# The expert loop's weights in fewer, larger transfers, in another order

## The chip, the cores and the metric

The kernel runs on one core of a Trainium2 chip. The metric is device time in microseconds. Engine names are those of the profile: PE is TensorE's matmul, PEld its weight load, DVE VectorE, ACT ScalarE, POOL GpSimd, SP SyncE; SPq is SyncE's sequencer, which issues transfers.

## The reference

One layer of a backbone over 2048 latent tokens of 1024 columns and 256 context tokens: an input projection, neighbourhood attention in 8 heads, a bidirectional mLSTM in 4 heads, an output projection, and a mixture of 64 experts, of which each token uses two. All in float32. The change touches how the experts' weights come in (and, for their room, how attention names its tiles). What the experts compute:

```python
def expert_block(args):
    tok, e = args
    xb = xt[jnp.minimum(tok, n_tok - 1)]
    return (jax.nn.silu(xb @ w1[e]) * (xb @ w3[e])) @ w2[e]     # w1, w3: 1024x512, w2: 512x1024
```

An expert's three matrices are 2.1 MB each, 6.29 MB together, and 64 experts are 403 MB.

## The kernel before, in words

The kernel runs its stages one after another: input projection, mLSTM, attention, output projection with routing, the expert loop, a last normalisation. Attention keeps each head's operands in one of two pools: per head the tiles q, ka and kb (query, key high and low part) and bias0, bias1, bias2, each with three bias blocks. The output projection puts its weights into the even pool's tiles once they are free, and the expert loop then uses the same memory for expert weights.

The loop takes the experts' tokens in units. Each of its 28 iterations has two half-steps (u = 0 and u = 1), 56 in all, counted here from 0. A half-step computes one unit of the **wide lane** (64 tokens of an expert with many, `l = 0`) and one of the **narrow lane** (32 tokens, `l = 1`). On TensorE its order is: `hidden(1, u)`, the narrow unit's products with w1 and w3 in eight steps k of 128 rows; `hidden(0, u)`, the wide unit's (L2011 both); the transposes of the next tokens (L1975); `output(1, u)` and `output(0, u)`, the products with w2 in four pieces c (L2043). The result is scattered by GpSimd with an accumulating indirect transfer (L2054).

The wide lane has one set of weights, `W[0]`: w1 and w3 in the tiles mask (k 0 to 3), q (k 4, 5) and ka (k 6, 7), w2 in mo, mo, mo, xo. The narrow lane has two, used in turn: `W[1]` for u = 0 (kb, bias0, bias1, bias2; xo, xo, w2_1_2, w2_1_3) and `W[2]` for u = 1 (tiles w13_2_* and w2_2_*, shown as w). In half-step h SyncE issues the loads of the wide lane's next weights, which half-step h+1 uses, and of the narrow lane's, which half-step h+2 uses. A load waits until TensorE has read the old contents of its tile. Each has a condition: where the next unit belongs to the same expert, the transfer is left out, but the instruction still stands in SyncE's queue, makes its waits, and then counts its completion semaphore up itself, for TensorE waits on that all the same.

SyncE works in order. Its order in a half-step was: the narrow lane's first half of w1 and w3 (four transfers of 0.52 MB, `load13`, L1097), the wide lane's first half (four), the narrow lane's second half (four), the wide lane's second half (four), then w2 of the narrow lane (four, `load2`, L1102) and of the wide lane (four): 24. The scheduler gives SyncE's transfers eight completion semaphores in rotation, and a transfer waits until the one that had its semaphore before has landed. With 24 in a half-step, the four narrow ones of a group always share their semaphores with the narrow groups before and behind them. Which expert comes next SyncE reads from a table in SBUF (`coming`, TENSOR_LOAD, two values for each lane).

```python
                e1, f1 = coming(1, u)
                e0, f0 = coming(0, u)
                for c in (0, 2):
                    load13(e1, (c, c + 1), f1)
                    load13(e0, (c, c + 1), f0)
                ...
                load2(e1, f1)
                load2(e0, f0)
```

Of the kernel before, what the change touches and what calls it, by code (L numbers as in the profile page):

```python
# [35 lines left out]
def tile_layer(ctx, tc, A, out):  # L36
# [666 lines left out]
    def head(h):  # L703

        pair, f0 = h // 2, (h % 2) * 64
        kp = kps[h % 2]
        q = kp.tile([P, SEQ], F32R, name="q")
        ka = kp.tile([P, NT], F32R, name="ka")
        kb = kp.tile([P, NT], F32R, name="kb")
        load(q[0:64, :].bitcast(F32), qhi_d[pair][f0 : f0 + 64, :])  # L710
        yield
        load(q[64:P, :].bitcast(F32), qlo_d[pair][f0 : f0 + 64, :])
        yield
        for dst, src in ((ka, khi_d), (kb, klo_d)):
            for p0 in (0, 64):
                load(dst[p0 : p0 + 64, :].bitcast(F32), src[pair][f0 : f0 + 64, :])
            yield
        bias = []

        def masked(i):  # L720
            w = (12, 16, 12)[i // 3] * 32
            in_order(nc.gpsimd.tensor_tensor(bias[i][:, 0:w], bias[i][:, 0:w], mask[:, i, 0:w], OP.add))  # L722

        for i in range(9):
            rt, ct = i // 3, i % 3
            if ct == 0:
# [4 lines left out]
            t = t3[:, ct, :]  # L731
# [177 lines left out]
    with ExitStack() as es:  # L909
# [12 lines left out]
        def out_weights(k):  # L922

            raw = raws[k]
            if k % 2 == 0:
                n_ = ("mask", "q", "ka", "kb")[k // 2]
                if n_ == "mask":
                    pair_ = kps[0].tile([P, 4, D], F32R, name=n_)
                    spare.append(pair_)
                else:  # L930
                    pair_ = kps[0].tile([P, 2, D], F32R, name=n_)
                pairs.append(pair_)
            hi, lo = pairs[k // 2][:, 0], pairs[k // 2][:, 1]
            if k % 2:
                if k == 1:
                    hi, lo = pairs[0][:, 2], pairs[0][:, 3]
                else:
                    t3 = kps[0].tile([P, 2, D], F32R, name=f"bias{k // 2 - 1}")
                    hi, lo = t3[:, 0], t3[:, 1]
            in_order(nc.scalar.copy(hi, raw[:]))  # L940
# [4 lines left out]

        pairs, spare, raws = [], [], []

# [151 lines left out]
    def load2(e, fl=None, chunks=range(4)):  # L1099
        for i in chunks:  # L1100
            s_ = A["w2"][0, e[0], i * P : (i + 1) * P, :].rearrange("o p n -> p (o n)")
            in_order(nc.sync.dma_start(e[1][1][i][:], s_, cond=fl))  # L1102

# [4 lines left out]
    with ExitStack() as es:  # L1108
# [517 lines left out]
        def first_rows(l, chunks):  # L1626
# [3 lines left out]
            for c in chunks:  # L1630
                W[l][1].append(xi.tile([P, D], F32, name="mo" if l == 0 and c < 3 else "xo"))
            load2(ahead_[l], chunks=chunks)

# [46 lines left out]

        both_ = kps[0].tile([P, 2, 2, 2, 512], F32, name="mask")
        for l, tags in enumerate((("q", "ka"), ("kb", "bias0", "bias1", "bias2"))):
            w13 = [both_[:, 0], both_[:, 1]] if l == 0 else []
            w13 += [kps[0].tile([P, 2, 2, 512], F32, name=n)[:] for n in tags]
            W[l][0].extend(w13)
        for e in ahead_:
            load13(e, range(4))
        first_rows(1, (1,))
# [53 lines left out]
    with ExitStack() as es:  # L1742
        sp = es.enter_context(tc.tile_pool(name="ro_s", bufs=1, reuse_waits="tile"))
        pp = es.enter_context(tc.tile_pool(name="ro_p", bufs=1, space=PSUM, reuse_waits="tile"))
        load2(ahead_[1], chunks=(2, 3))
        e = (ds(nc.values_load(fi[0:1, 2:3], engines=SPE, min_val=0, max_val=63), 1), W[2])
        load13(e, range(4))
        for l, G, c0 in ((0, 2, 0), (1, 4, 512)):
# [205 lines left out]
    wp = moe.enter_context(tc.tile_pool(name="mo_w2", bufs=1, reuse_waits="tile"))  # L1954
    W[2][1].extend(wp.tile([P, D], F32, name=f"w2_2_{i}") for i in range(4))
    load2(e)


    with ExitStack() as es:
# [37 lines left out]
        with tc.For_i(0, n_it, 1, iteration_sync="reg_based") as it:  # L1997
# [3 lines left out]
            def hidden(l, u, between=None):  # L2001
                n, t0 = ((64, 0), (32, 64))[l]
                G = P // n
                w13 = W[0 if l == 0 else 1 + u][0]
                NH = 512 // G
                ph = pp.tile([P, 2, NH], F32, name=f"ph{l}")
                for k in range(KC):
                    if k == 4 and between:
                        between()
                    for j in range(G):  # L2010
                        in_order(nc.tensor.matmul(  # L2011
                            ph[j * n : (j + 1) * n], xT[u][:, k, t0 : t0 + n], w13[k // 2][:, :, k % 2, j * NH : (j + 1) * NH],
                            start=k == 0, stop=k == KC - 1, tile_position=(0, j * n),
                        ))
# [15 lines left out]
            def output(l, u, m, part=None):  # L2030
# [3 lines left out]
                NY = D // G  # L2034
                w2t = W[0 if l == 0 else 1 + u][1]
                gT = gts[l, u]
# [39 lines left out]
            for u in range(2):  # L2076
# [146 lines left out]
```

## Time and profile before

| | us |
|---|---|
| median of 3 runs | 2878.04 (2877.48 to 2882.16) |
| the profiled execution: time | 2883.94 |
| the profiled execution: span | 2882.1 |
| TensorE busy in it | 2525.8 |
| the expert loop in it, first to last product | 1158.8 (1649.1 to 2807.9) |

The span is the time from the first to the last instruction of the profiled execution, the time is what the device counted for the same execution. Times in rows are microseconds from the span's start. A row of a timeline joins several instructions of the same kind; its second number runs from the first one's start to the last one's end.

### The profile page before, as it was taken

The numbers are of one execution on the slowest core, as the hardware profiler recorded it, in microseconds if no ns is written. First come the engines' busy times: TensorE is split into PE (matmuls) and PEld (weight loads), VectorE is DVE, ScalarE is ACT, GpSimd is POOL, SyncE is SP. The second block draws the span as 40 slices with busy tenths as digits, with TensorE's granted clock in tenths as the row PEclk, the third lists the DMA queues.
The fourth block names the chain that finished last, engine by engine and source line by source line (L and its number), as shares of the span: only waits on it lengthen the run. The fifth ranks groups of instructions, "written<-read, shape, count | busy, mean of one in ns | idle before, by whom it ended". The sixth has DMA issues, their size and how long they took to land. (4 is left out here: it accounts for less than half of the span.)

```text
span 2882.1 us, 53652 instructions
## 1 busy us (share of the span) xinstructions
PE 2525.8 (88%) x17276; PEld 1592.8 (55%) x17276; DVE 1235.1 (43%) x2493; ACT 782.0 (27%) x1693; POOL 862.5 (30%) x927
## 2 busy tenths in 40 slices
PE   8999999999977999988988498978998999979890
PEld 4878578777877777776766333323333333323330
DVE  5456135274159865656799721111211211211125
ACT  4333115242145655554543200000000000000004
POOL 1202210011145345455766421212221222212126
PEclk9999999999989999999999599989999999989895
DMA  8634853335299777877544899999597888988926
GB/s 269 163 114 133 276 166 109 121 118 161 93 215 267 203 172 187 187 186 196 149 126 123 271 326 317 312 351 303 168 330 254 272 277 250 339 284 266 338 77 248
DMA packets 361806, 628.05 MB, mean 218 GB/s; under 512 B 82680, under 2 KB 146156, under 8 KB 358604
## 3 DMA queue, kind: packets, MB, share of 16 engines
q1 hardware_dynamic: 329868, 565.92, 61.5%
q0 software_dynamic: 31216, 60.03, 9.2%
q8 instruction: 70, 1.15, 0.2%
q10 hardware_dynamic: 592, 0.46, 0.1%
q14 instruction: 60, 0.49, 0.1%
HBM read 948.05 MB, written 97.42 MB: 363 GB/s over the span
## 5 line engine op out<-in xcount | busy, mean ns | idle before, releaser
L2054 POOL DMA_INDIRECT acc_d<-y,ids x112 | 174.3, 1557 | 670.9 <-DVE y L2051 363.5
L2011 PE MATMUL ph<-mask,xT 128*64 128x512 f32 x896 | 219.3, 632 | 53.6 <-DMA mask<-in_w_dram 53.5
L2017 DVE TENSOR_TENSOR sg<-sg,ph 128x128 f32<-128x128 f32 x112 | 39.6, 354 | 512.3 <-ACT sg L2016 512.3
L2016 ACT ACTIVATE sg<-ph 128x128 f32<-128x128 f32 x112 | 37.0, 330 | 801.2 <-PE ph L2011 590.3
L246 PE MATMUL ps<-xhi,whi 128*128 128x512 f32 (+1 forms) x576 | 221.7, 386 | 1.6 <-DVE ev L509 1.6
L248 PE MATMUL ps<-xhi,wlo 128*128 128x512 f32 (+1 forms) x576 | 220.2, 382 | 0.2 <-DVE wlo L235 0.2
L247 PE MATMUL ps<-xlo,whi 128*128 128x512 f32 (+1 forms) x576 | 220.4, 383 | 0.0
L2011 PE MATMUL ph<-q,xT 128*64 128x512 f32 x448 | 125.3, 685 | 55.7 <-DMA q<-in_w_dram 55.5
L255 PE MATMUL ps<-whi,xhi 128*128 128x512 f32 x416 | 166.1, 400 | 1.4 <-ACT whi L234 1.4
L256 PE MATMUL ps<-wlo,xhi 128*128 128x512 f32 x416 | 164.3, 396 | 3.1 <-DVE wlo L235 3.1
L2011 PEld LDWEIGHTS ph<-mask,xT 128*64 128x64 f32 x896 | 65.3, 143 | 182.4 <-issue 177.3
L972 DVE CUSTOM_DVE_ANT_0 sb<-ps,bias 128x640 f32<-128x640 f32 (+1 forms) x128 | 113.9, 890 | 121.3 <-PE ps L969 106.7
L257 PE MATMUL ps<-whi,xlo 128*128 128x512 f32 x416 | 164.8, 397 | 0.0
L2043 PE MATMUL py<-mo,gT 128*64 128x512 f32 x672 | 158.3, 601 | 6.1 <-DMA mo<-in_w_dram 4.7
L2051 DVE SCALAR_TENSOR_TENSOR y<-py,wgt,g2r 128x256 f32<-128x256 f32 x112 | 69.1, 617 | 220.4 <-PE py L2043 220.4
L1967 POOL DMA_INDIRECT xb<-h_d,idg x58 | 58.1, 1002 | 273.9 <-PE py L2043 251.2
L2027 DVE COPY gT<-pg 128x128 f32<-128x128 f32 x112 | 40.1, 358 | 212.7 <-PE pg L2025 211.5
L246 PEld LDWEIGHTS ps<-xhi,whi 128*128 128x128 f32 x576 | 108.3, 188 | 28.4 <-issue 3.2
L248 PEld LDWEIGHTS ps<-xhi,wlo 128*128 128x128 f32 x576 | 108.3, 188 | 23.3 <-DVE wlo L235 0.6
L247 PEld LDWEIGHTS ps<-xlo,whi 128*128 128x128 f32 x576 | 108.4, 188 | 22.7 <-DVE xlo L182 0.5
L980 ACT ACTIVATE sb<-sb,nm 128x640 f32<-128x640 f32 (+1 forms) x128 | 113.2, 884 | 19.1 <-DVE nm L972 15.3
L722 POOL TENSOR_TENSOR bias<-bias,mask 128x384 f32<-128x384 f32 (+1 forms) x72 | 78.1, 1100 | 119.3 <-DMA bias<-rel_d 119.3
(576 smaller groups left out, 5361.7 us busy)
## 6 DMA issues: line engine op xcount, KB each, us to landing
w<-in_w_dram SPq DMA_DIRECT2D x406, 512.0 KB, 8.1
mask<-in_w_dram SPq DMA_DIRECT2D x228, 512.0 KB, 6.3
bias<-in_w_dram SPq DMA_DIRECT2D x174, 512.0 KB, 11.3
mo<-in_w_dram SPq DMA_DIRECT2D x171, 512.0 KB
xo<-in_w_dram SPq DMA_DIRECT2D x115, 512.0 KB
q<-in_w_dram SPq DMA_DIRECT2D x114, 512.0 KB
ka<-in_w_dram SPq DMA_DIRECT2D x114, 512.0 KB
kb<-in_w_dram SPq DMA_DIRECT2D x58, 512.0 KB
```

What stands on the lines that cost most here:

```text
L246: nc.tensor.matmul(ps, wh_, xhi[g, k][:], start=k == 0, stop=False)
L247: nc.tensor.matmul(ps, wh_, xlo[g, k][:], start=False, stop=False)
L248: nc.tensor.matmul(ps, wl_, xhi[g, k][:], start=False, stop=k == KC - 1)
L255: nc.tensor.matmul(ps, xh, his[k], start=k == 0, stop=False)
L256: nc.tensor.matmul(ps, xh, los[k], start=False, stop=False)
L257: nc.tensor.matmul(ps, xl, his[k], start=False, stop=k == KC - 1)
L722: in_order(nc.gpsimd.tensor_tensor(bias[i][:, 0:w], bias[i][:, 0:w], mask[:, i, 0:w], OP.add))
L972: in_order(nc.vector.tensor_tensor_reduce(out=sb[:, 0:L], in0=ps[:, off:768], in1=bt[:, 0:L], scale=-0.125, scalar=3.0e38, op0=OP.add, op1 ...
L980: in_order(nc.scalar.activation(sb[:, 0:L], sb[:, 0:L], AF.Exp, bias=nm[:], scale=-1.0, accum_out=rss[n // 8][:, n % 8 : n % 8 + 1]))
L2011: in_order(nc.tensor.matmul(ph[j * n : (j + 1) * n], xT[u][:, k, t0 : t0 + n], w13[k // 2][:, :, k % 2, j * NH : (j + 1) * NH], start=k == ...
L2043: in_order(nc.tensor.matmul(py[j * n : (j + 1) * n, :], gT[:, b_, j_ * n : (j_ + 1) * n], w2t[c][:, j * NY : (j + 1) * NY], start=c == 0, ...
L2054: sc = nc.gpsimd.indirect_dma_start(out=acc_d[:].rearrange("t (g n) -> (t g) n", g=G), out_offset=bass.IndirectOffsetOnAxis(ap=ids[u][:, l ...
```

## The change

Attention's q, ka and kb become one tile qkk of the same size, and bias0 to bias2 one tile bias. With these the expert lanes' weights lie in larger pieces. The wide lane's w1 and w3 are two pieces of four k (mask, and the first part of qkk) in place of one of four k loaded in two parts and two of two k. `W[1]` has one piece of four k (bias) and two of two k (bias, and the rest of qkk), with the last two c of w2 in one piece. `W[2]` has two pieces of four k and two w2 pieces of two c. A transfer carries one matrix of one piece: 1.05 MB for four k or for two c. The wide lane's w2 stays in four. A half-step issues 17 transfers at u = 0 (nine narrow, eight wide) and 14 at u = 1 (six and eight), 31 an iteration in place of 48. The wide lane's w1 and w3 now stand as a whole behind the narrow lane's first piece, and the narrow lane's other pieces behind them. The loads ahead of the loop are cut in the same way.

```diff
@@ attention, head(h) @@
-        q = kp.tile([P, SEQ], F32R, name="q")
-        ka = kp.tile([P, NT], F32R, name="ka")
-        kb = kp.tile([P, NT], F32R, name="kb")
+        qkk = kp.tile([P, SEQ + 2 * NT], F32R, name="qkk")
+        q, ka, kb = qkk[:, 0:SEQ], qkk[:, SEQ : SEQ + NT], qkk[:, SEQ + NT :]
...
-            if ct == 0:
-                t3 = kp.tile([P, 3, 768], F32, name=f"bias{rt}")
+            if i == 0:
+                b9 = kp.tile([P, 9, 768], F32, name="bias")
...
@@ load13, load2 @@
-        for i in chunks:
+
+        k = 0
+        for i, t in enumerate(e[1][0]):
+            n = t.shape[2]
             for q, src in enumerate(("w1", "w3")):
-                s_ = A[src][0, e[0], i * 256 : (i + 1) * 256, :].rearrange("o (k p) n -> p (o k) n", p=P)
-                in_order(nc.sync.dma_start(e[1][0][i][:, q], s_, cond=fl))
...
+                if i in chunks:
+                    s_ = A[src][0, e[0], k * P : (k + n) * P, :].rearrange("o (k p) n -> p (o k) n", p=P)
+                    in_order(nc.sync.dma_start(t[:, q], s_, cond=fl))
+            k += n
...
@@ the lanes' tiles @@
-        both_ = kps[0].tile([P, 2, 2, 2, 512], F32, name="mask")
-        for l, tags in enumerate((("q", "ka"), ("kb", "bias0", "bias1", "bias2"))):
-            w13 = [both_[:, 0], both_[:, 1]] if l == 0 else []
-            w13 += [kps[0].tile([P, 2, 2, 512], F32, name=n)[:] for n in tags]
-            W[l][0].extend(w13)
+        m_, q_, b_ = (kps[0].tile([P, n * 1024], F32, name=t) for t, n in (("mask", 4), ("qkk", 6), ("bias", 6)))
+        for l, t, k, n in ((0, m_, 0, 4), (0, q_, 0, 4), (1, b_, 0, 4), (1, b_, 4, 2), (1, q_, 4, 2)):
+            W[l][0].append(t[:, k * 1024 : (k + n) * 1024].rearrange("p (q k n) -> p q k n", q=2, n=512))
...
-    W.append(([wp.tile([P, 2, 2, 512], F32, name=f"w13_2_{i}") for i in range(4)], []))
-    W[1][1].extend(wp.tile([P, D], F32, name=f"w2_1_{i}") for i in range(2, 4))
+    W.append(([wp.tile([P, 2, 4, 512], F32, name=f"w13_2_{i}")[:] for i in range(2)], []))
+    W[1][1].append(wp.tile([P, 2, D], F32, name="w2_1")[:])
...
-    W[2][1].extend(wp.tile([P, D], F32, name=f"w2_2_{i}") for i in range(4))
+    W[2][1].extend(wp.tile([P, 2, D], F32, name=f"w2_2_{i}")[:] for i in range(2))
...
@@ the loop @@
                 e1, f1 = coming(1, u)
+                load13(e1, (0,), f1)
                 e0, f0 = coming(0, u)
-                for c in (0, 2):
-                    load13(e1, (c, c + 1), f1)
-                    load13(e0, (c, c + 1), f0)
+                load13(e0, (0, 1), f0)
+                load13(e1, (1, 2), f1)
```

SyncE's queue shows both halves of the edit. First the w1 and w3 loads of a half-step with u = 0, from the end of the narrow lane's first piece on (kb and bias are narrow, mask and q wide; ISA and REGISTER_ALU set registers). Before:

```order
L1097 DMA bias_14485<-in_w_dram 128x2x512
L1097 ISA
L1097 DMA mask<-in_w_dram 128x2x512
L1097 ISA
L1097 DMA mask<-in_w_dram 128x2x512
L1097 ISA
L1097 DMA mask<-in_w_dram 128x2x512
L1097 ISA
L1097 DMA mask<-in_w_dram 128x2x512
L1097 ISA
L1097 DMA bias_14486<-in_w_dram 128x2x512
```

The same place in the changed kernel (its load13 is at L1089; bias is narrow, mask and qkk wide, until the second bias):

```order
L1089 DMA bias<-in_w_dram 128x4x512
L1089 ISA
L1089 DMA mask<-in_w_dram 128x4x512
L1089 ISA
L1089 DMA mask<-in_w_dram 128x4x512
L1089 ISA
L1089 REGISTER_ALU
L1089 DMA qkk<-in_w_dram 128x4x512
L1089 ISA
L1089 DMA qkk<-in_w_dram 128x4x512
L1089 ISA
L1089 DMA bias<-in_w_dram 128x2x512
```

Four transfers between the narrow lane's pieces were half of the wide lane's w1 and w3, and four are now all of it.

Second, where u = 0 ends and u = 1 begins in SyncE's queue (xo is the last piece of the wide lane's w2, w_2_0 the first of the narrow lane's at u = 1). Before:

```order
L1102 DMA xo<-in_w_dram 128x1024
L2073 ISA
L2073 TENSOR_LOAD items
L2073 ISA x2
L2072 ISA
L2072 TENSOR_LOAD items
L2072 ISA x2
L2073 ISA
L2073 TENSOR_LOAD items
L2073 ISA x2
L1097 ISA
L1097 DMA w_2_0_14713<-in_w_dram 128x2x512
```

In the changed kernel:

```order
L1099 REGISTER_ALU
L1099 DMA xo<-in_w_dram 128x1024
L1089 ISA
L1089 DMA w_2_0_14667<-in_w_dram 128x4x512
L1089 ISA
L1089 DMA w_2_0_14667<-in_w_dram 128x4x512
```

The three table reads that stood between the half-steps have gone to the iteration's head, where all eight now stand before the first transfer (five did).

## Rows read from the trace of the kernel before

**Rows 1.** The page: busy time by engine, then two lines of the span in 40 slices of 72 us: the busy tenths of TensorE and the mean busy tenths of the 16 DMA engines.

```profile
PE 2525.8 (88%) x17276; PEld 1592.8 (55%) x17276; DVE 1235.1 (43%) x2493; ACT 782.0 (27%) x1693; POOL 862.5 (30%) x927
...
PE   8999999999977999988988498978998999979890
...
DMA  8634853335299777877544899999597888988926
```

**Rows 2.** Busy time of each engine by window (us; PE, PEld, DVE, ACT, POOL), then the granted TensorE clock as a share of full speed, the DMA engines' mean busy share and GB/s. The first two are the loop's first and last stretch, the other three lie inside the loop.

```profile
1649.00:1997.00 348.00, 303.89 (x2480) 119.86 (x2480) 60.02 (x160) 20.83 (x40) 64.27 (x47) 0.93 0.95 322
...
2650.00:2808.00 158.00, 135.03 (x1085) 52.20 (x1077) 26.50 (x70) 8.47 (x17) 27.80 (x20) 0.91 0.67 221
1850.00:1900.00 50.00, 34.58 (x276) 13.50 (x276) 5.98 (x16) 2.60 (x5) 6.68 (x5) 0.86 1.01 350
2550.00:2600.00 50.00, 33.51 (x277) 12.94 (x277) 7.00 (x18) 1.07 (x4) 6.13 (x5) 0.80 1.02 360
1660.00:1760.00 100.00, 99.01 (x859) 39.37 (x859) 21.74 (x57) 6.25 (x13) 22.14 (x16) 1.00 0.98 325
```

**Rows 3.** TensorE in order of time at chosen places (start us, us, engine, line, operation out<-in, shapes, count): the first product of half-steps 0, 16, 17, 18, 25, 31, 38, 44 and 49 (nine of 56), and the last products of the loop.

```profile
1649.08 1.93 PE L2011 MATMUL ph<-kb,xT 128*32 128x256 f32 x16 [1.05 <-DVE xT L1978]
...
1997.42 0.85 PE L2011 MATMUL ph<-kb,xT 128*32 128x256 f32 x12
...
2015.20 1.07 PE L2011 MATMUL ph<-w,xT 128*32 128x256 f32 x16
...
2032.98 1.07 PE L2011 MATMUL ph<-kb,xT 128*32 128x256 f32 x16
...
2164.32 1.06 PE L2011 MATMUL ph<-w,xT 128*32 128x256 f32 x14
...
2285.05 1.29 PE L2011 MATMUL ph<-w,xT 128*32 128x256 f32 x20
...
2418.06 1.07 PE L2011 MATMUL ph<-kb,xT 128*32 128x256 f32 x16
...
2538.59 1.07 PE L2011 MATMUL ph<-kb,xT 128*32 128x256 f32 x16
...
2649.84 1.50 PE L2011 MATMUL ph<-w,xT 128*32 128x256 f32 x24
...
2806.82 1.03 PE L2043 MATMUL py<-xo,gT 128*64 128x512 f32 x4
```

**Rows 4.** Who waited for whom in the loop, 1649 to 2808 us: TensorE's three longest waits for transfers (us in total, times, longest us).

```profile
PE ph L2011 <- DMA q<-in_w_dram: 55.5, 17, 7.9
PE ph L2011 <- DMA mask<-in_w_dram: 53.5, 19, 11.2
...
PEld ph L2011 <- DMA q<-in_w_dram: 31.9, 12, 4.6
```

**Rows 5.** SyncE's DMA queue in order of time in half-steps 3 to 5 (start us, us from the first issue to the end of the last, count). On L1097 w is of the narrow lane, mask and q of the wide one; on L1102 xo x1 is the wide lane's last piece; kb is the narrow lane's first piece of half-step 4.

```profile
1717.99 2.61 SPq L1097 DMA_DIRECT2D w<-in_w_dram  x4
1720.99 1.42 SPq L1097 DMA_DIRECT2D mask<-in_w_dram  x4
1722.89 4.17 SPq L1097 DMA_DIRECT2D w<-in_w_dram  x4
...
1734.56 0.07 SPq L1102 DMA_DIRECT2D xo<-in_w_dram  x1
1739.03 1.08 SPq L1097 DMA_DIRECT2D kb<-in_w_dram  x2
...
1757.30 0.07 SPq L1102 DMA_DIRECT2D xo<-in_w_dram  x1
1759.84 2.61 SPq L1097 DMA_DIRECT2D w<-in_w_dram  x4
...
1764.74 6.02 SPq L1097 DMA_DIRECT2D w<-in_w_dram  x4
1771.21 0.50 SPq L1097 DMA_DIRECT2D q<-in_w_dram  x2
```

**Rows 6.** TensorE in half-step 6 (the bracket is idle time before, and what ended it).

```profile
1763.43 3.65 PE L2011 MATMUL ph<-mask,xT 128*64 128x512 f32 x16 [0.26 <-DMA mask<-in_w_dram]
...
1771.83 3.68 PE L2011 MATMUL ph<-q,xT 128*64 128x512 f32 x8 [4.49 <-DMA q<-in_w_dram]
```

**Rows 7.** SyncE's own waits in the loop: the longest in total (us in total, times, longest us).

```profile
SPq L1097 <- DMA w<-in_w_dram: 45.1, 59, 2.3
```

**Rows 8.** The wide lane around half-step 38: its first product on TensorE, SyncE's issue of the next weights into the same tile, and the first wide product of half-step 39.

```profile
2421.66 2.79 PE L2011 MATMUL ph<-mask,xT 128*64 128x512 f32 x12
...
2438.92 2.50 SPq L1097 DMA_DIRECT2D mask<-in_w_dram  x4
...
2444.70 3.68 PE L2011 MATMUL ph<-mask,xT 128*64 128x512 f32 x8 [5.18 <-DMA mask<-in_w_dram]
```

**Rows 9.** SyncE's issue of the wide lane's first pieces in the first and the last of the seven half-steps in which they are loaded (10, 14, 22, 25, 38, 44, 49).

```profile
1872.69 2.61 SPq L1097 DMA_DIRECT2D mask<-in_w_dram  x4
...
2676.11 2.73 SPq L1097 DMA_DIRECT2D mask<-in_w_dram  x4
```

**Rows 10.** DMA queues in the loop, 1649 to 2808 us: packets, MB, share of 16 engines (q1 is SyncE's, q0 that of the indirect transfers).

```profile
q1 hardware_dynamic: 126940, 290.69, 70.1%
q0 software_dynamic: 22295, 33.18, 14.6%
```

More of the change, by code (lines that the diff above doesn't have):

```diff
@@ L730, in head @@
             off = rel.offset + ((ct * 16) * 8 + h) * 23 * 32 + i0 * 32
-            t = t3[:, ct, :]
+            t = b9[:, i, :]
             in_order(nc.gpsimd.memset(t[:, nr * 32 :], 0.0))
@@ L924, in out_weights @@
             raw = raws[k]
[L925 to L939, printed above, removed]
+            if k in (0, 2, 5):
+                t = kps[0].tile([P, 3 if k else 2, 2, D], F32R, name={0: "mask", 2: "qkk", 5: "bias"}[k])
+                pairs.extend((t[:, i, 0], t[:, i, 1]) for i in range(t.shape[1]))
+            hi, lo = pairs[k]
             in_order(nc.scalar.copy(hi, raw[:]))
@@ L944, in low_part @@
             in_order((nc.gpsimd, nc.vector)[k % 2].tensor_tensor(wlo[KO[k]], raws[k][:], whi[KO[k]].bitcast(F32), OP.subtract))
-        pairs, spare, raws = [], [], []
+        pairs, raws = [], []
         def raw_weights(k):
@@ L1093, in load13, with load2 @@
     def load13(e, chunks, fl=None):
-        for i in chunks:
+        k = 0
+        for i, t in enumerate(e[1][0]):
+            n = t.shape[2]
             for q, src in enumerate(("w1", "w3")):
-                s_ = A[src][0, e[0], i * 256 : (i + 1) * 256, :].rearrange("o (k p) n -> p (o k) n", p=P)
-                in_order(nc.sync.dma_start(e[1][0][i][:, q], s_, cond=fl))
[L1099 to L1102, printed above, removed]
+                if i in chunks:
+                    s_ = A[src][0, e[0], k * P : (k + n) * P, :].rearrange("o (k p) n -> p (o k) n", p=P)
+                    in_order(nc.sync.dma_start(t[:, q], s_, cond=fl))
+            k += n
+    def load2(e, fl=None, pieces=range(4)):
+        c = 0
+        for i, t in enumerate(e[1][1]):
+            n = t.shape[1]
+            if i in pieces:
+                s_ = A["w2"][0, e[0], c * P : (c + n) * P, :].rearrange("o (c p) n -> p (o c) n", p=P)
+                in_order(nc.sync.dma_start(t, s_, cond=fl))
+            c += n
     ro_es = ExitStack()
@@ L1630, in first_rows @@
             for c in chunks:
-                W[l][1].append(xi.tile([P, D], F32, name="mo" if l == 0 and c < 3 else "xo"))
-            load2(ahead_[l], chunks=chunks)
+                W[l][1].append(xi.tile([P, 1, D], F32, name="mo" if l == 0 and c < 3 else "xo")[:])
+            load2(ahead_[l], pieces=chunks)
         ahead_ = []
@@ L1679, in tile_layer @@
                 first_experts()
-        both_ = kps[0].tile([P, 2, 2, 2, 512], F32, name="mask")
-        for l, tags in enumerate((("q", "ka"), ("kb", "bias0", "bias1", "bias2"))):
-            w13 = [both_[:, 0], both_[:, 1]] if l == 0 else []
-            w13 += [kps[0].tile([P, 2, 2, 512], F32, name=n)[:] for n in tags]
-            W[l][0].extend(w13)
+        m_, q_, b_ = (kps[0].tile([P, n * 1024], F32, name=t) for t, n in (("mask", 4), ("qkk", 6), ("bias", 6)))
+        for l, t, k, n in ((0, m_, 0, 4), (0, q_, 0, 4), (1, b_, 0, 4), (1, b_, 4, 2), (1, q_, 4, 2)):
+            W[l][0].append(t[:, k * 1024 : (k + n) * 1024].rearrange("p (q k n) -> p q k n", q=2, n=512))
         for e in ahead_:
-            load13(e, range(4))
+            load13(e, range(3))
         first_rows(1, (1,))
@@ L1744, in tile_layer @@
         pp = es.enter_context(tc.tile_pool(name="ro_p", bufs=1, space=PSUM, reuse_waits="tile"))
-        load2(ahead_[1], chunks=(2, 3))
+        load2(ahead_[1], pieces=(2,))
         e = (ds(nc.values_load(fi[0:1, 2:3], engines=SPE, min_val=0, max_val=63), 1), W[2])
-        load13(e, range(4))
+        load13(e, range(2))
         for l, G, c0 in ((0, 2, 0), (1, 4, 512)):
@@ L2003, in hidden @@
                 G = P // n
-                w13 = W[0 if l == 0 else 1 + u][0]
+                w13 = [t[:, :, k] for t in W[0 if l == 0 else 1 + u][0] for k in range(t.shape[2])]
                 NH = 512 // G
@@ L2011, in hidden @@
                         in_order(nc.tensor.matmul(
-                            ph[j * n : (j + 1) * n], xT[u][:, k, t0 : t0 + n], w13[k // 2][:, :, k % 2, j * NH : (j + 1) * NH],
+                            ph[j * n : (j + 1) * n], xT[u][:, k, t0 : t0 + n], w13[k][:, :, j * NH : (j + 1) * NH],
                             start=k == 0, stop=k == KC - 1, tile_position=(0, j * n),
@@ L2034, in output @@
                 NY = D // G
-                w2t = W[0 if l == 0 else 1 + u][1]
+                w2t = [t[:, i] for t in W[0 if l == 0 else 1 + u][1] for i in range(t.shape[1])]
                 gT = gts[l, u]
```

## The prediction

> **What bounds the kernel now.** I read the page first, then windows, then single waits. The page says that TensorE is busy for 88% of the span and that in the loop, from slice 22 on, the DMA engines are at eight or nine tenths in most slices [rows 1]. Neither is full, so the question is what each waits for. The starts of the half-steps answer it [rows 3]: half-step 17 takes 2032.98 - 2015.20 = 17.78 us, which is TensorE's own pace, and 56 of them would be 995.7 us. The loop takes from 1649.1 to 2807.9, 1158.8 us. So **163 us** are lost in it. From the same rows, each stretch less 17.78 us for each half-step: A (0 to 15) 63.8, B (16 to 24) 6.9, C (25 to 30) 14.1, D (31 to 37) 8.6, E (38 to 43) 13.9, F (44 to 48) 22.4, G (49 to 55) 33.5.
>
> The waits name the cause [rows 4]: nearly all are for q and mask, the wide lane's w1 and w3. Yet the wide lane is loaded in only seven half-steps (SyncE's issues tell it: four loaded ones of mask take 2.6 or 2.7 us [rows 9], four left out 1.42 [rows 5]). Over the whole loop SyncE's queue moves 290.7 MB [rows 10], 46 loads of 6.29 MB: 39 narrow, 7 wide. Half-step 6 shows how a load that moves nothing stalls TensorE. SyncE gets to q of half-step 5 at 1771.21, only because four narrow transfers stand before it and take from 1764.74 on, and TensorE resumes at 1771.83 after 4.49 us idle [rows 5, 6]. The reader should see there that SyncE is **late**: it comes to q when TensorE already stands at it in the next half-step.
>
> Why it is late: in half-steps 3 and 4, with narrow loads alone, it needs 21.0 us a turn (1717.99, 1739.03, 1759.84 [rows 5]), where TensorE needs 17.78. Its own work is the larger part. Four loaded issues take 1720.99 - 1717.99 = 3.0 us, 0.75 each; four left out take 1.42 from the first one's start to the last one's end, (1.42 - 0.07) / 3 = 0.45 each, 0.07 being the one left out alone at 1734.56; the gaps with the table reads are 1739.03 - 1734.56 = 4.5 and 1759.84 - 1757.30 = 2.5 us. An iteration has 24 x 0.75 + 24 x 0.45 + 7.0 = 35.8 us of this, 17.9 a half-step, and the rest, 3 us, is waiting for transfers: its three longest kinds of wait are for narrow loads, led by 45.1 us in 59 times [rows 7]. As narrow groups share four semaphores, each narrow transfer waits for the fourth narrow one before it, so 2.1 MB are under way at most.
>
> **The change, part by part.**
>
> *Fewer issues.* With narrow loads alone an iteration becomes 15 x 0.75 + 16 x 0.45 + 7.0 = 25.5 us, 12.7 a half-step, 5.1 less, and below 17.78. SyncE then runs with TensorE until transfers hold it. A 1.05 MB issue is not in the trace; I take 0.75 for it (below: nothing excludes 0.7, above: twice, 1.5, which gives an iteration of up to 36.7 us and SyncE as late as now).
>
> *Order.* The wide lane's first issue stands behind two narrow ones, and a left-out q no longer stands behind a whole narrow w1 and w3. The rotation over eight stays, but with 17 and 14 the groups no longer meet on the same four semaphores, so 4 MB and more can be under way. One wait remains: a wide first piece gets the semaphores of the last narrow w2 transfers of the half-step before, so it waits for that load's end.
>
> *What this is worth.* I go by bytes, since SyncE no longer decides. A load is 6.29 MB and the indirect transfers are 33.2 / 56 = 0.59 MB a half-step [rows 10]. The rate is not known for the new sizes. Below: 325 GB/s, the window of narrow loads alone [rows 2], 19.4 us a load and 1.8 for the scatter. Above: 350, the lower of two windows with wide and narrow loads together, where eight transfers are under way (the other has 360), 18.0 and 1.7. Each stretch at 350, and at 325:
> A: SyncE's issues give 14 narrow and 2 wide loads whose arrival half-step 15 needs, less 6.0 us for the last w2: 16 x 18.0 + 15 x 1.7 - 6.0 = 307.5 us. It starts 8 us after 1649.1 (7.0 of reads, all at the head now, and 1.0 to the first byte). Behind the last byte 1.0 us of signalling and 10.4 of products remain: 17.78 less 3.65 for mask [rows 6] and less the narrow lane's 3.6, from 2418.06 [rows 3] to 2421.66 [rows 8]. The end is at 1976 and not 1997.4: 21.5 us gained. At 325: nothing.
> B, D, E: one wide load each in B and E, none in D. Half-step 38 shows what is lost: its first mask product starts at 2421.66, SyncE's issue comes 17.3 us later, and half-step 39 begins its wide lane at 2444.70 after 5.18 us idle [rows 8]. Issued when the piece is free, 3.7 us after its first product, and with up to 2 us of the narrow load before it, the two pieces are there after 3.7 + 2 + 12.0 + 1.0 = 18.7 us; the first is wanted after 17.78, and needs only half of these bytes. All of it goes: 6.9 + 8.6 + 13.9 = 29.4, by either rate.
> C: both lanes at half-step 25. 4 us to the first byte, two loads and the scatter 39.4, 1.9 for the signal and the last w2 product: 45.3 for two half-steps, 9.7 over 35.56, so 4.4 gained (1.5).
> F: a narrow load goes before, 5.9 us into half-step 44; 47.2 us for two half-steps, 11.6 over, 10.8 gained (6.4).
> G: with half-steps 47 and 48 before it, four loads: 4 + 72 + 6.8 + 1.9 = 84.7 for four half-steps, 13.6 over 71.1, 19.9 gained (14.1).
> Sum: **86** at 350 and **51** at 325. I take the middle, 69, because stretch A is of the narrow kind while C, F and G are of the other.
>
> *Larger pieces.* A piece of 2.1 MB must land whole before its first product, and after it four k remain and not two: 1.9 us (half of mask's 3.65, [rows 6]) in each of four stalls that stay, -7 (below: 0; above: also 3.0 us for the extra 1.05 MB at 350, in seven wide loads, -34). Earlier freeing is lost too, 1.8 us a piece, but while SyncE came 17 us late that was no cover anyone used.
>
> *At nothing.* The joined attention tiles: the loads of a head start only after the last scores of the head two before, as each old tile's last reader was in that last block too. If that were wrong, each of six heads would start its loads later by what one bias tile had been free earlier. The loads before the loop: the loop's first product waits for DVE and not for a transfer, as the bracket at 1649.08 has it [rows 3].
>
> 2883.9 - 69 + 7 = 2822 for the profiled execution; this stood 5.9 over the median, so **2816** for the median.
>
> [...]
>
> **The rivals.**
> *Bytes alone bound it.* In stretch A the DMA engines are 95% busy, in the narrow window 98% [rows 2], so SyncE may be late because it waits for them. For it: the waits of [rows 7]. Against it: stretch G with 67%, and the stall of 39. Then B, D and E keep their losses, A gives nothing, and only the order at double loads (C, F, G at 325: 22) remains: about 2856.
> *Slower.* The large pieces decide: SyncE stays late, since issue time grows with size, and every wide load must come whole. Price: 7 x (3.0 + 1.9 + 1.8) = 47, so 2925 with no gain beside it. It decides if SyncE still issues mask over about 12 us after its first product. Against it: four loaded issues of w13 took 3.0 us at 0.52 MB, which is time per instruction as much as per byte.
> *More.* The DMA engines run well above 360 GB/s with more under way and slack carries over between stretches: waits of 40 remain of 163, 2878 - 123 = 2755.
> *It does not do what it says.* A semaphore rotation that still ties wide to narrow makes it the same as before, 2878.
>
> **How the numbers follow.** The forecast has 0.70, with a range of its own from 2783 to 2845 (86 and a little over, 51 less the 7 and a little under). Bytes alone 0.11, more 0.06, no change 0.05, slower 0.08. A measurement can tell about 0.2%, 6 us, from no change. Faster is 0.70 + 0.11 + 0.06 = 0.87, same 0.05, slower 0.08. The range goes from 2783 to 2862, to where the low sum meets the dear end of the larger pieces (51 - 34 = 17, 2861) and past "bytes alone"; it leaves out the slower case, no change and most of "more".
>
> **What would show it.** Right: SyncE's turn in half-steps 3 to 5 at 17.8 to 20 us; its wide issue under 10 us after the first wide product where no load is behind; B, D and E at 17.78 us a half-step; waits for q and mask under 60 us in all; the window from 1660 to 1760 nearer 350 GB/s. Wrong: a loaded 1.05 MB issue of over 1.2 us, a rate still at 325 in stretch A, or long waits of SyncE for w2 transfers before it issues mask.

## The result and the profile after

The changed kernel takes **2806.6 us** (median of 4 runs, 2802.4 to 2816.2) beside 2880.1 of the kernel before on the same chip: ratio 0.9751, 95% interval 0.9724 to 0.9778. That is 73.5 us less; 2816 was forecast. The profiled execution went from 2883.9 to 2809.5.

The page of the changed kernel: busy time by engine, TensorE's and the DMA engines' busy tenths in 40 slices of 70 us. They answer to [rows 1].

```profile
PE 2503.2 (89%) x17276; PEld 1578.5 (56%) x17276; DVE 1236.0 (44%) x2493; ACT 782.0 (28%) x1693; POOL 860.6 (31%) x927
...
PE   8999999999987899988988679978998999999890
...
DMA  8634752434379788876544679999789887999926
```

The work is the same and TensorE's busy time nearly so. The first product of half-steps 0, 16, 25, 31, 38, 44 and 49 and the last products of the loop, as in [rows 3]:

```profile
1644.50 1.93 PE L2007 MATMUL ph<-bias,xT 128*32 128x256 f32 x16 [1.05 <-DVE xT L1974]
...
1971.90 1.29 PE L2007 MATMUL ph<-bias,xT 128*32 128x256 f32 x20
...
2135.11 1.07 PE L2007 MATMUL ph<-w,xT 128*32 128x256 f32 x16
...
2254.92 1.29 PE L2007 MATMUL ph<-w,xT 128*32 128x256 f32 x20
...
2379.40 1.29 PE L2007 MATMUL ph<-bias,xT 128*32 128x256 f32 x20
...
2488.31 1.50 PE L2007 MATMUL ph<-bias,xT 128*32 128x256 f32 x24
...
2592.47 1.72 PE L2007 MATMUL ph<-w,xT 128*32 128x256 f32 x28
...
2732.33 1.03 PE L2039 MATMUL py<-xo,gT 128*64 128x512 f32 x4
```

The loop takes 2733.4 - 1644.5 = 1088.9 us where it took 1158.8: 69.9 us gained there, and 74.2 us followed it before, 74.4 now. The other 4.6 us lie ahead of the loop, and no run shows them to be an effect of the change: the loop starts anywhere between 1642.9 and 1652.8 in the eleven experiments below, and the two of them with the old attention tiles (1643.8, 1644.7) start as early as any. By stretch, time lost against 17.78 us a half-step:

| stretch | lost before | lost after | gained | forecast at 350 / 325 GB/s |
|---|---|---|---|---|
| A, half-steps 0 to 15 | 63.8 | 42.9 | 20.9 | 21.5 / 0 |
| B, D, E | 29.4 | 5.4 | 24.0 | 29.4 / 29.4 |
| C, 25 to 30 | 14.1 | 13.1 | 1.0 | 4.4 / 1.5 |
| F, 44 to 48 | 22.4 | 15.3 | 7.1 | 10.8 / 6.4 |
| G, 49 to 55 | 33.5 | 16.4 | 17.1 | 19.9 / 14.1 |

Windows of the changed kernel (columns as in [rows 2]): the first and the last stretch, the two with wide and narrow loads together, and the one with narrow loads alone.

```profile
1644.00:1972.00 328.00, 297.31 (x2484) 116.40 (x2488) 60.49 (x160) 20.82 (x40) 64.26 (x47) 0.93 1.00 344
2592.00:2734.00 142.00, 130.64 (x1089) 50.37 (x1085) 27.01 (x70) 8.47 (x17) 28.23 (x21) 0.95 0.68 229
1660.00:1760.00 100.00, 100.00 (x889) 39.72 (x887) 21.46 (x58) 7.43 (x14) 22.81 (x17) 1.00 1.01 351
1845.00:1895.00 50.00, 33.35 (x252) 12.48 (x250) 5.10 (x13) 2.22 (x4) 7.22 (x5) 0.80 1.04 375
2505.00:2555.00 50.00, 39.64 (x308) 15.29 (x306) 7.59 (x20) 2.60 (x5) 7.70 (x6) 0.86 1.04 371
```

With narrow loads alone the DMA engines now move 351 GB/s where they moved 325, at a busy share of 1.01 where it was 0.98: in stretch A **they** are full. (The share alone does not prove it; the extra reads below have 0.99 at 329 GB/s.) The granted clock is 0.93 in A, as before. It is 1.00 from 1660 to 1760, where TensorE never stands, and 0.80 and 0.86 in the two windows around the long stalls of half-steps 11 and 45: the longest stalls stay, and there the granted clock is 0.50 of full speed for some microseconds (from 1855.0 to 1868.5 and from 2513.8 to 2520.5, and the 16 products on mask that run then take 6.18 and 6.33 us and not 3.65).

TensorE's waits for transfers in the loop of the changed kernel, as in [rows 4]:

```profile
PE ph L2007 <- DMA mask<-in_w_dram: 38.7, 8, 12.6
PE py L2039 <- DMA mask<-in_w_dram: 14.2, 2, 8.5
PE py L2039 <- DMA mo<-in_w_dram: 9.2, 3, 5.0
PE ph L2007 <- DMA qkk<-in_w_dram: 4.8, 4, 1.6
```

Waits for w1 and w3 of the wide lane fell from 140.9 us in 48 times [rows 4] to 43.5 in 12. The half-steps over 17.8 us are now 11, 15, 23, 26, 39, 45 and 50, each right behind a wide load, and 0, 9 and 43 with 2.8, 4.3 and 1.4 us. What has grown is the wait at the output products (py) for the wide lane's w2: 4.7 us in 9 times before (tile mo), 23.4 in 5 now (the two rows of py; the bracket of the first names another transfer of the same load).

SyncE's queue in half-steps 4 and 5, as in [rows 5] (on L1089 bias, w and the qkk that follows bias are narrow; mask and the qkk that follows mask are the left-out wide ones; on L1099 xo and w are narrow until mo comes):

```profile
1729.76 1.05 SPq L1089 DMA_DIRECT2D bias<-in_w_dram  x2
1735.06 0.52 SPq L1089 DMA_DIRECT2D mask<-in_w_dram  x2
1736.05 0.53 SPq L1089 DMA_DIRECT2D qkk<-in_w_dram  x2
1736.91 1.07 SPq L1089 DMA_DIRECT2D bias<-in_w_dram  x2
1738.30 4.04 SPq L1089 DMA_DIRECT2D qkk<-in_w_dram  x2
...
1746.77 0.07 SPq L1099 DMA_DIRECT2D xo<-in_w_dram  x1
1747.43 2.37 SPq L1089 DMA_DIRECT2D w<-in_w_dram  x2
...
1762.08 0.07 SPq L1099 DMA_DIRECT2D xo<-in_w_dram  x1
1768.61 2.28 SPq L1089 DMA_DIRECT2D bias<-in_w_dram  x2
```

Two issues of 1.05 MB take 1.05 us from the first's start to the second's end, and two of 0.52 MB took 1.08 [rows 5]: an issue costs about the same at either size here. SyncE still needs 19.4 us a half-step here ((1768.61 - 1729.76) / 2), but much of it is now waiting: 4.04 us for two issues, say, since the second takes the semaphore (137) of a narrow transfer not yet landed: that one lands at 1741.94 and the issue starts at 1741.96.

### The profile page after: what moved, and what is told of

Same layout as the page of the kernel before. It is cut to its first block, busy times and chain, and to the rows that moved or that the text cites. A ratio compares the mean times of both kernels' runs of the same rounds, so it can differ in the third digit from the quotient of the medians.

```text
span 2807.7 us, 50968 instructions
## 1 busy us (share of the span) xinstructions
PE 2503.2 (89%) x17276; PEld 1578.5 (56%) x17276; DVE 1236.0 (44%) x2493; ACT 782.0 (28%) x1693; POOL 860.6 (31%) x927
## 5 line engine op out<-in xcount | busy, mean ns | idle before, releaser
L2007 PE MATMUL ph<-mask,xT 128*64 128x512 f32 x896 | 217.0, 629 | 38.7 <-DMA mask<-in_w_dram 38.7
L2007 PE MATMUL ph<-qkk,xT 128*64 128x512 f32 (+1 forms) x1344 | 234.2, 526 | 4.8 <-DMA qkk<-in_w_dram 4.8
L2039 PE MATMUL py<-mo,gT 128*64 128x512 f32 x672 | 166.3, 632 | 23.4 <-DMA mask<-in_w_dram 14.2
L2007 PEld LDWEIGHTS ph<-qkk,xT 128*64 128x64 f32 (+1 forms) x1344 | 75.1, 128 | 116.9 <-issue 101.2
L968 ACT ACTIVATE sb<-sb,nm 128x640 f32<-128x640 f32 (+1 forms) x128 | 113.2, 884 | 18.9 <-DVE nm L960 15.0
## 6 DMA issues: line engine op xcount, KB each, us to landing
w<-in_w_dram SPq DMA_DIRECT2D x203, 1024.0 KB, 10.8
```

Of the source, the lines that this page charges most:

```text
L968: in_order(nc.scalar.activation(sb[:, 0:L], sb[:, 0:L], AF.Exp, bias=nm[:], scale=-1.0, accum_out=rss[n // 8][:, n % 8 : n % 8 + 1]))
L2007: in_order(nc.tensor.matmul(ph[j * n : (j + 1) * n], xT[u][:, k, t0 : t0 + n], w13[k][:, :, j * NH : (j + 1) * NH], start=k == 0, stop=k = ...
L2039: in_order(nc.tensor.matmul(py[j * n : (j + 1) * n, :], gT[:, b_, j_ * n : (j_ + 1) * n], w2t[c][:, j * NY : (j + 1) * NY], start=c == 0, ...
```

## The experiments

Four theories stood against each other. **1**: SyncE's own issuing time makes loads late. **2**: the order of the issues does. **3**: larger transfers run at a higher rate. **4**, formed after the first four runs: the completion semaphores, eight taken in turn, tie a transfer to the eighth issue before it, left out or not. Times are medians, each measured beside the kernel before; for comparisons between experiments that were measured apart the ratio to it is used, one per cent being 29 us.

**The order alone**, in the kernel before:

```diff
-                for c in (0, 2):
-                    load13(e1, (c, c + 1), f1)
-                    load13(e0, (c, c + 1), f0)
+                load13(e1, (0, 1), f1)
+                load13(e0, range(4), f0)
+                load13(e1, (2, 3), f1)
```

> The kernel before with the new order alone: per half-step the narrow lane's first four pieces of w1 and w3, then all eight of the wide lane, then the narrow lane's other four; 24 issues of 0.52 MB as before, tiles as before. Theory 1 (SyncE's own time, 17.9 us of issuing a half-step against TensorE's 17.78, makes the loads late): the number of issues is unchanged, so most of the loss stays; the wide lane's last pieces come four issues sooner and the narrow groups no longer share four semaphores, which is worth 10 to 25 us: 2855 to 2870 us. Theory 2 (the order is what counts): nearly the whole gain, 2806 to 2820 us. Theory 3 (only the size of a transfer counts, by the rate): no change, 2875 to 2885 us.

Measured: 2912.9 beside 2885.0, ratio 1.0099 (1.0061 to 1.0136): **slower** by 28 us. No theory had that. The order that the change brings is harmful where the pieces are small.

**The sizes alone**: the changed kernel with `load13(e1, (0,)); load13(e0, (0,)); load13(e1, (1, 2)); load13(e0, (1,))`.

> The changed kernel with the order of before: narrow half, wide half, narrow half, wide half, in the larger transfers (17 and 14 issues a half-step). Theory 1 (SyncE's own time): 12.7 us of issuing a half-step remain, so nearly the whole gain stays: 2805 to 2820 us. Theory 2 (the order is what counts): little of it stays, 2855 to 2875 us. Theory 3 (the rate of larger transfers): the rate of the first 16 half-steps stays near 344 GB/s, 2806 to 2815 us.

Measured: 2813.8, ratio 0.9746 (0.9729 to 0.9764), the same as the whole change. Theory 2 falls: at these sizes the order is worth nothing that the ratios show.

**Narrow pieces small again** (new tiles, new order; in `load13` and `load2` the loop's narrow tiles are cut):

```diff
+            m = 2 if fl is not None and e[1] is not W[0] else n
+            for j in range(0, n, m):
```

> The changed kernel (tiles and order) with the narrow lane's loads in the loop cut into 0.52 MB pieces again: 20 issues a half-step, 12 of them narrow, the wide lane's w1 and w3 still 4 of 1.05 MB. Theory 1 (SyncE's own time): about 0.6 us for each of the 9 added issues of an iteration gives 15.5 us a half-step, still under 17.78 but with less slack after a wide load: 2810 to 2825 us. Theory 3 (the rate of larger transfers): almost all loaded bytes are narrow, so the first 16 half-steps go back to about 325 GB/s and lose 20 us: 2826 to 2840 us.

Measured: 2836.3, ratio 0.9824 (0.9805 to 0.9842). About 21 us by the ratios (30 by the medians) of the gain are gone, 51 stay. The window from 1660 to 1760 has 317 GB/s, but at a DMA share of 0.96, so the engines were not full; this alone does not part theory 1 from theory 3. The time lies in theory 3's range and not in theory 1's; but four narrow pieces beside four left-out wide issues now hold 2.1 MB, where up to twice that stood, so theory 4 may have a part in it too. Stretch A loses 54.7 us here, 11.8 more than in the changed kernel. What the size itself gives can be read in the trace: from 1660 to 1960 SyncE's queue moved 90.09 MB at 83.7% of the 16 engines' time before the change, 93.00 at 86.4% here and 96.48 at 88.3% in the changed kernel, so the larger transfers took 1.5% less engine time per byte.

**Wide pieces small again** (the same cut for `e[1] is W[0]`; 49 of 56 times these transfers are left out):

> The changed kernel with the wide lane's w1 and w3 cut into eight 0.52 MB pieces again (they are left out in 49 of 56 half-steps): 21 and 18 issues a half-step. Theory 1 (SyncE's own time, left-out issues too): 4 left-out issues at 0.45 us more in a half-step, 14.6 us in all, under 17.78: 2808 to 2818 us, the loss in half-steps behind a wide load. Theory 3 (the rate of larger transfers): the narrow bytes go as in the changed kernel, no change beyond 3 us: 2804 to 2810 us.

Measured: 2903.4, ratio 1.0065 (1.0044 to 1.0086): slower than the kernel before, though it has 39 issues an iteration and that one 48. Neither theory had it within 80 us. The trace shows why. SyncE's queue in half-steps 2 and 3 of this kernel:

```profile
1700.65 1.06 SPq L1091 DMA_DIRECT2D bias<-in_w_dram  x2
1706.11 1.27 SPq L1091 DMA_DIRECT2D mask<-in_w_dram  x4
1707.76 5.34 SPq L1091 DMA_DIRECT2D qkk<-in_w_dram  x4
1713.41 1.08 SPq L1091 DMA_DIRECT2D bias<-in_w_dram  x2
```

and the same stretch issue by issue from the trace's records (start us, tile, number of the completion semaphore, landing of a loaded one, wait ahead of the issue):

```
1700.65 bias  136  lands 1710.39
1701.32 bias  137  lands 1713.00
1706.11 mask  138  left out
 (138 to 143: mask x4, qkk x2, left out)
1710.52 qkk   136  left out, after 1.89 us for semaphore 136
1713.02 qkk   137  left out, after 2.14 us for semaphore 137
1713.41 bias  138  loaded
```

The eighth issue after a loaded one, left out though it is, takes its semaphore and waits until it has landed. With eight in a row, SyncE reaches the next narrow piece at 1713.41, when the two under way have **both** landed, the last at 1713.00: nothing more of the narrow lane is in flight then. The window from 1660 to 1760 of this kernel, with the DMA engines at 0.88:

```profile
1660.00:1760.00 100.00, 94.38 (x788) 37.01 (x786) 19.31 (x51) 5.87 (x12) 20.60 (x15) 0.97 0.88 296
```

The order alone puts the same eight in a row (share 0.92, 312 GB/s in that window). This is theory 4, and the next run was made for it.

**The same transfers in the old order**: as before, with the four lines of the sizes-alone kernel, so that at most four left-out ones of w1 and w3 stand in a row.

> The same transfers as wide_small (wide lane's w1 and w3 in eight pieces, 21 and 18 issues a half-step), in the order of the kernel before: narrow half, wide half, narrow half, wide half. Theory 4, made after the first four runs: the eight completion semaphores are taken in turn, by left-out transfers too, so the bytes under way are those of the narrow pieces among the last eight issues; in wide_small eight left-out issues in a row left none. Here every eight issues in a row hold at least 2.1 MB of narrow pieces: 2810 to 2835 us. Theory 1 (SyncE's own issuing time alone): it is that of wide_small, so the time is too, 2895 to 2910 us.

Measured: 2820.5, ratio 0.9779 (0.9736 to 0.9821). Number, size and kind of the transfers are those of the kernel before it, only the order differs, and 83 us lie between the medians. Theory 4 is **shown**: in these kernels what stands among the eight last issues decides what is under way.

**More of SyncE's own time**: two more pairs of table reads at each `coming`, whose values nothing uses.

> The changed kernel with 16 more table reads in an iteration on SyncE, whose values nothing uses; no transfer differs. By the 7.0 us that eight reads took, some 14 us more of SyncE's own time in an iteration: 12.7 + 7 = 19.7 us a half-step, over TensorE's 17.78. Theory 1 (SyncE's own time): in half-steps where SyncE does not wait for transfers anyway it comes late again, 2830 to 2900 us. Theory 4 alone (only bytes under way by the semaphores count): within 5 us of the changed kernel, 2802 to 2812 us.

Measured: 2870.5, ratio 0.9969 (0.9948 to 0.999). No transfer and no semaphore differs, yet about 63 of the 72 us are gone, by the ratios. The reads' gaps sum to 18.9 us an iteration (6.4 in the changed kernel), 6.2 us a half-step more, so with narrow loads alone its own turn is about 18.7, over TensorE's 17.78. SyncE's waits for TensorE to have read the w1 and w3 in a tile (us in total, times, longest), in the changed kernel and then here:

```profile
SPq L1089 <- PE ph L2007: 78.8, 37, 4.4
```

```profile
SPq L1089 <- PE ph L2007: 7.1, 10, 2.9
```

In the changed kernel SyncE often comes to a tile before it is free, here seldom: it is the late one. TensorE's waits for mask went from 38.7 us in 8 times to

```profile
PE ph L2007 <- DMA mask<-in_w_dram: 93.5, 20, 13.7
```

Theory 1 is shown too: SyncE's own time over 17.78 us a half-step brings the stalls back with nothing else changed. By stretch, B, D and E lose 37.3 us (5.4 in the changed kernel, 29.4 in the kernel before), but A only 48.8 (42.9, 63.8). So in A some 15 of the 20.9 us gained stay although SyncE is late: there its own time is not the whole cause, and no run separates what more bytes under way give from what larger pieces give. Nor does the size of the transfers alone keep the rate, as theory 3 would have it. The window from 1660 to 1760 here, with the changed kernel's transfers, where that one has 351 GB/s:

```profile
1660.00:1760.00 100.00, 97.64 (x877) 39.00 (x873) 21.10 (x57) 6.17 (x13) 22.79 (x17) 1.00 0.99 329
```

**The wide lane's issues on ScalarE**, in the kernel before, so that left-out ones leave SyncE's line:

```diff
+                in_order((nc.scalar if fl is not None and e[1] is W[0] else nc.sync).dma_start(...))
```

> The kernel before, sizes, tiles and order as they were, but the wide lane's loads in the loop (and its two table reads) are issued by ScalarE, so SyncE issues only the narrow lane's 12 a half-step, about 9 us, and left-out wide transfers take none of its semaphores. Theory 4 with theory 1 (the left-out transfers in SyncE's line are what costs, by its time and its semaphores): 2800 to 2825 us with the small transfers. Theory 3 (the rate of larger transfers): the 0.52 MB pieces keep the rate of the first 16 half-steps at 325 GB/s, 2850 to 2880 us.

Measured: 2873.7, ratio 0.9967 (0.9947 to 0.9987): 10 us, not 60. The stall moved. TensorE's waits for mask are down to 4.3 us, but in its loop stand now (TensorE, then ScalarE):

```profile
PE pg L2026 <- DVE sg L2018: 121.6, 27, 20.2
...
ACT L2017 <- DMA bias<-in_w_dram: 119.2, 8, 16.7
```

The eight semaphores serve both queues: in the records ScalarE's transfers take 137, 139, 141 and 143 in 616 of 671 issues, and some left-out ones wait for narrow ones under way (bias). ScalarE's activation stands behind them and TensorE behind that. SyncE's take the other four in 616 of 672, so with pieces of 0.52 MB still only about 2.1 MB can be under way. The time lies in theory 3's range, but as a test of theory 1 or 3 it is inconclusive, since it brought a wait of its own.

**The wide w2 ahead of the narrow one**, in the changed kernel: `load2(e0, f0)` before `load2(e1, f1)`.

> The changed kernel with the wide lane's w2 issued before the narrow lane's w2 of the same half-step. The wide lane's weights are needed one half-step on, the narrow lane's two, and TensorE's last waits in the changed kernel stand behind wide loads (half-steps 11, 15, 26, 45, 50: 80 us in all). If the place in the line sets when a transfer lands, the wide w2 lands up to 6 us sooner in the five half-steps outside the first 16: 2785 to 2800 us. If the bytes set it whatever the order: 2802 to 2810 us. If holding the narrow w2 back until the wide product has been read drains the transfers under way in the half-steps without a wide load: 2812 to 2830 us.

Measured: 2796.3, ratio 0.9703 (0.9661 to 0.9745); its interval overlaps that of the changed kernel, so the stalls decide. In half-step 26 of the changed kernel TensorE waits for the wide w2 (tile mo; the bracket names another transfer of the same load); below it the same place here:

```profile
2177.85 5.15 PE L2039 MATMUL py<-mo,gT 128*64 128x512 f32 x12 [8.52 <-DMA mask<-in_w_dram]
```

```profile
2171.79 2.30 PE L2039 MATMUL py<-mo,gT 128*64 128x512 f32 x8 [0.21 <-DMA mo<-in_w_dram]
```

Half-step 26 falls from 30.9 to 19.0 us, 45 from 33.0 to 25.5, 50 from 34.1 to 29.5; 53 rises from 17.8 to 23.3, where narrow weights come late in turn. In stretch A the loss goes from 42.9 to 45.5: there order buys nothing, since the bytes bound it.

**All wide issues first.**

> The changed kernel with all of the wide lane's issues ahead of the narrow lane's of the same half-step, w1 and w3 as well as w2. If what w2_swap gained (11 us on medians) comes from the wide lane's earlier place, the 2.1 MB of narrow w1 and w3 that still stand ahead of it are worth up to 6 us in each of half-steps 45 and 50: 2785 to 2796 us. If the narrow pieces, held back until the wide product has been read, leave the DMA engines empty in half-steps without a wide load: 2800 to 2830 us.

Measured: 2815.7 (2802.9 to 2818.8), ratio 0.9795 (0.9777 to 0.9814), by the ratios 13 us slower than the changed kernel, with intervals that just meet. Its profiled execution, span 2801.1 us, is the fastest of its five, with a loop of 1084.4 us beside the changed kernel's 1088.9, and does not show where these 13 us go; that stays open.

**Longer rows**, to see whether the DMA engines bound stretch A:

```diff
-s_ = A[src][0, e[0], k * P : (k + n) * P, :].rearrange("o (k p) n -> p (o k) n", p=P)
+s_ = A[src][0, e[0], :, :].rearrange("o (p k) n -> p (o k) n", p=P)[:, k : k + n, :]
-xb[u][:, k * P : (k + 1) * P]
+xb[u][:, k : k + (P - 1) * KC + 1 : KC]
```

> The changed kernel with the rows of w1 and w3 dealt to partitions the other way round (partition p holds rows 8p to 8p+7, and the transposes of x take every eighth column), so that a transfer of four chunks is one piece of 8 KB a partition and not four of 2 KB; number and order of the issues as they are. Packets of 2 KB took 84 ns and of 4 KB 160 ns in the trace of before, 24.4 and 25.6 bytes per ns. If the changed kernel's first 16 half-steps are bound by the DMA engines (their share is 1.00 there), 3 to 5 per cent of their 327 us come back and some of the other stalls: 2785 to 2800 us. If something else (SyncE, the memory itself) bounds them: 2802 to 2812 us.

Measured: 2801.7, ratio 0.9738 (0.9718 to 0.9757). By the ratios that is no difference that can be told from the changed kernel, and it lies between the two expected ranges. The DMA queue of SyncE from 1660 to 1960 us, in the changed kernel and then here (packets, MB, share of 16 engines):

```profile
q1 hardware_dynamic: 41264, 96.48, 88.3%
```

```profile
q1 hardware_dynamic: 19502, 98.30, 85.1%
```

2% more bytes in 4% less of the engines' time: 5.4% per byte. In the profiled executions A's loss against 17.78 us falls by 10.1 us, although every half-step now takes 18.03, since a transpose of every eighth column takes 284 ns and not 253:

```profile
L1971 PE MATMUL pxt<-ident,xb 96*128 96x96 f32 x448 | 63.2, 284 | 0.0
```

```profile
L1971 PE MATMUL pxt<-ident,xb 96*128 96x96 f32 x448 | 49.3, 253 | 0.0
```

(here, then in the changed kernel). That speaks for the engines as the bound of A. The whole loop is 12.0 us shorter in the profiled execution (1076.9 beside 1088.9), with 14 us of dearer transposes in it (56 x 0.25, 4 of them in A); but it starts 8.3 us later, inside the scatter of these starts, which hides most of that in the total.

**Both**, wide w2 first and longer rows:

> Both that and the wide w2 ahead of the narrow one. If the two gains add: 2775 to 2790 us. If they save the same waits: 2790 to 2798 us.

Measured: **2775.5 us**, ratio 0.9656 (0.9627 to 0.9685), faster than both kernels of this case, by the ratios 27 us under the change (31 by the medians). That is in the range for gains that add; in the profiled executions the loop is 16.8 and 12.0 us shorter with one of them. In the profiled execution with both it takes 1055.7 us, 33 less than in the changed kernel; its waits for mask are 28.8 us in 5 times, for mo 1.1.

## Why the prediction was right, point by point

- **SyncE late by its own time: right**, and shown by the extra reads, for the larger part of the gain: outside A they undo all of it, in A about 6 of 20.9 us. 6.2 us more a half-step on SyncE cost about 63 us. An issue of 0.75 us stood against 1.5 us for 0.52 MB at 350 GB/s, and one left out took 0.45 us with no DMA beside it [rows 2, 5]; even so SyncE's time made the loads late.
- **An issue of 1.05 MB at 0.75 us: right.** Two take 1.05 us end to end, 0.67 from one to the next.
- **The semaphores: seen but not weighed.** The prediction named the rotation and said that the groups would no longer meet on four semaphores. It didn't see that the new order, with small wide pieces, would leave none to the narrow lane: the order alone is 28 us slower. In these runs it is harmless only with the wide w1 and w3 in four transfers. Order and size, written down as two gains, are one gain and a condition for it.
- **Stretch A: right at the upper end.** 20.9 of 21.5 us at a measured 351 GB/s; the middle between 350 and 325 was too careful by 10 us. The rate was taken from a window of another kind, with wide loads. The two terms of 1.0 us, to the first byte and for the signal behind the last, can be read in the records of the kernel before, at the 21 places in the loop where SyncE's queue ran empty for over 1.2 us: the first packet started 1.04 to 1.07 us after its issue (once 1.42), and the last count of a semaphore came 0.33 to 0.99 us after the last packet's end, 0.61 in the median; TensorE's product followed 0.14 us after that count at 2444.70 (half-step 39). So the first term was right, and the second, at 0.5 to 1.1 us, was near its upper end. Of the causes given, SyncE's time is worth about 6 us here by the extra reads; how the rest divides between more bytes under way and larger pieces stays open.
- **B, D and E: 24.0 of 29.4.** D goes to 124.5 us, 17.78 a half-step. Left are mainly half-step 23 with 3.2 us, and 39 and 43 with 0.9 and 1.4. The step that failed is "issued when the piece is free, 3.7 us after its first product": in half-step 22 SyncE comes 8.0 us after it. It had ended half-step 21's issues 0.2 us before that product, and then the eight table reads, now all at the iteration's head, and two left-out narrow issues stood before mask.
- **C, F and G: 25.2, inside the forecast's 35.1 and 22.0**, near its lower end, although the rate behind the wide load of F was 371 GB/s. C got 1.0 us and not 1.5 to 4.4. The end of these stalls was taken as the last byte of both loads in any order; the wide w2, issued last, ends the stall in 26, and issuing it earlier took 11.9 us out of that half-step.
- **Larger pieces, -7: not found.** The stretches sum to 70.1 us, with this loss in it, against 69 forecast without. With wide pieces of 0.52 MB in the same order C, F and G lose 47.4 us, with 1.05 MB 44.3 (the old order's two kernels): smaller pieces shorten no stall. This term, less 7 with an end at less 34, is the one mis-sized. (The 34 counts 1.9 us in all seven wide loads, where the text beside it names four stalls; with four it is 29.)
- **The total: right in part by luck.** The stretches gave 70.1 us for 69 forecast, but A gave 10 more than the middle taken and the others 9 less, and these errors cancel. For the profiled execution 2822 was forecast and 2809.5 measured: about 7 of the 12.5 us is the term for larger pieces, 4.6 the loop's earlier start, which lies within the scatter of these starts.
- **The joined attention tiles at nothing: not contradicted.** The loop's starts scatter over 10 us, and those of the kernels with the old tiles (1643.8, 1644.7, 1649.1) lie inside that, so a smaller cost would not show.
- **The rivals.** "Bytes alone bound it" (2856) fell, but it is true of what is left: stretch A is at a DMA share of 1.00. "Slower" fell at the issue time. "More" (2755) did not come: 93 of the 163 us stay, although the windows behind wide loads have 375 and 371 GB/s. "A rotation that still ties wide to narrow" was real, and near: the same change without the larger wide pieces measured 2903.
- Of the signs named, SyncE's turn in half-steps 3 to 5 is 19.8 us on average ((1768.61 - 1709.28) / 3), waits for w1 and w3 are 43.5 us in all, and the window from 1660 has 351 GB/s. D is at 17.78 us a half-step, B and E are 3.2 and 2.2 us over in all. SyncE's wide issue came 3.7 to 8.0 us after the first wide product in every half-step right behind one without a load; behind a load it came up to 19.7 us after it. One sign of being wrong showed in part: with u = 0 SyncE waited up to 4.3 us for the narrow w2 of the half-step before until it could issue mask, the wait that the prediction had named under the order.

## What to carry to other kernels

A transfer that a condition left out still cost its place here: about 0.45 us of the issuing engine and one of eight completion semaphores, and with eight left-out ones in a row the queue drained (a DMA share of 0.88 with the wide pieces small and 0.92 with the order alone from 1660 to 1760, beside 1.01 in the changed kernel). Count the issuing engine's time for a turn against the pace of the engine that it feeds, and lay the issues out so that each eight hold enough bytes that really move; larger pieces did both here. When TensorE then waits for bytes, put what is needed sooner ahead of what is needed later (11.9 us out of half-step 26 here, nothing in stretch A), and look at the packet's length (5.4% of the engines' time per byte here).

## What the runs showed of the hardware

An issue on SyncE took about the same time for 0.52 and 1.05 MB (two end to end 1.08 and 1.05 us). The eight semaphores were shared by two issuing queues with the wide issues on ScalarE (four of them in 616 of its 671 issues, the other four in 616 of SyncE's 672), and left-out transfers on ScalarE waited for ones under way on SyncE (ScalarE's activations stood until a narrow one, bias, had landed for 119.2 us in 8 times). Cutting SyncE's packets from 41264 to 19502 for about the same bytes saved 5.4% of the DMA engines' time per byte, and reading every eighth column made a transpose 12% longer (284 against 253 ns). In the window from 1660 to 1760 the DMA engines' busy share was 0.99 at 329 GB/s (extra reads) and 1.01 at 351 (the changed kernel).
